# A memory pair's fetches in one step, and its gate's tanh ordered behind an exponential

## The chip, the core and the metric

The kernel runs on one core of a Trainium2 chip. Five engines work side by side: TensorE (PE, matrix products; its weight loads are shown apart as PEld), VectorE (DVE), ScalarE (ACT), GpSimd (POOL) and SyncE (SP), which here only issues DMAs. Each engine takes its instructions from its own queue, in the queue's order. The metric is the device time of one launch in microseconds (us); the median of three runs of the kernel before is 2737.72 us, from 2735.97 to 2738.56.

## The reference

One layer of a hybrid encoder for a prompt of 2048 rows and for 8 decode requests of 16 rows, all of width 1024, in float32. What is computed:

```python
h = rms_norm(x, norm_g[0]);  z = h @ w_in
qa, ka, va, qb, kb, vb, ob, ib, fb = split(z)
att = rms_norm(band_attention(qa, ka, va, rel_table), g_att)      # 8 heads x 64
hb, (c1, n1, m1) = mlstm_sequence(qb, kb / sqrt(128), vb, ig, log_sigmoid(fb), c0, n0, m0)
hb = hb * rsqrt(mean(hb * hb, -1) + EPS)                          # 4 heads x 128
mlstm_out = hb * g_mlstm * sigmoid(ob)
x = x + rms_norm(concat(att, mlstm_out) @ w_out, norm_g[1])
x = x + rms_norm(conv_ffn(rms_norm(x, norm_g[2])), norm_g[3])
```

The part around the change is the mLSTM, a matrix memory `C` (128 x 128 for each head, with a normaliser column) that is carried from chunk to chunk. For each chunk the weights are exp(d - m), with d from the gates and m a running maximum; the chunk's result is its own part, `(q k^T * w) v`, plus the carried part, `q C`; and `C` is scaled and gets `(k w_s)^T v`. At the end each head's row is normalised and multiplied by its gain and by the output gate sigmoid(ob), which the kernel computes as (1 + tanh(ob / 2)) with the gain halved.

## The kernel before

**Stages.** First the combined projection: 14 column groups of `w_in` for the first half of the rows (prompt tiles 0 to 7 and the decode tile), then the same 14 for the second half (tiles 8 to 15). A float32 product is made of three products of rounded and residual parts (`mm3`, L111 to L113). Groups `va`, `qk` give the attention's values, queries and keys, groups `qb`, `vo` the memory's queries and keys (`qkbd` in DRAM) and its values and output gates (`vobd`). Then comes the output projection (`project`, L997 and on), whose rows are read back from `mixd` in DRAM (L1015), squared and summed (L1020), scaled (L1022) and transposed (L83), and then the feed-forward part, which takes the second half of the time. Its matrix products have their sums and products of blocks arranged so that seven take the place of eight; nothing of the change lies in it.

**Units beside the projection.** Attention and memory run in the gaps of the projection's products. Each is a stream of units, and a unit is a Python generator that issues some instructions at each step and yields an estimate of their cost. A `Pipe` (L155 and on) holds the live units of one stream; one step of a pipe starts the next unit, if any, and lets every live unit issue its next step. `pump` (called after every few projection products) steps the attention's pipe and the memory's pipe in turn as long as the estimated VectorE cost lags behind.

**The memory's units.** `mlstm(h, half)` treats one head and one half of the rows: 8 chunks of 128 rows in 4 pairs. For each pair there are `chunk(s, 0)`, `load` of the pair after it, `chunk(s, 1)` and an empty unit. With 4 heads and 2 halves there are 32 pairs and 64 chunks.

`load` (L690 to L706) has three steps. The first takes the tile `mb` and fetches the running maximum, broadcast to all partitions (L693). The second takes the tile `mqk` and fetches queries and keys (L697), takes the tile `mvo` and fetches values and output gate (L700), writes a column of ones into `mvo` on GpSimd (L701) and masks `mb` on GpSimd (L702). The third loads the head's gain, for the first pair only. The tiles `mb`, `mqk`, `mvo`, `num` have two buffers each.

`chunk(s, c)` (L708 to L741): the first step makes q k^T (L715) and the transposed keys (L83), the exponential of the masked `mb` on ScalarE into `w` (L718), the scaled keys `kw` on ScalarE (L720), and `w` times the scores on VectorE (L721). The second step has the three products (L727 to L729), the carried memory's update on VectorE (L730) and the pair's `num` on ScalarE and VectorE (L731, L732). After the second chunk a third step calls `finish_heads`.

`finish_heads` (L662 to L684): the norms (squares on ScalarE, L671; the power on GpSimd, L676), the output gate's tanh in place on ScalarE (L677), gate times gain on VectorE (L678), the normalised and gated rows on VectorE (L682, which is the last reader of `mvo`), and their store to `mixd` on SP's queue (L684).

`mlstm_sample(h)` treats the decode rows of a head in its own units `own`, `batches` and `finish`; the last calls `finish_heads` too, so that there are 32 + 4 tanhs.

**What sets the order.** The whole program is written under

```python
with tile.TileContext(nc, schedule_with_timeline_sim=True) as tc:
```

so the order in which the code issues is not the order of the queues. A planner takes the instructions with their dependences, gives those that the code issues earlier the higher rank, simulates the engines with its own durations, and puts into each engine's queue whatever is ready in its simulation. Instructions of different units so change places, and a DMA whose buffer is not yet released is planned for the time when it will be. Once planned, a queue's order is fixed, and the chip keeps to it: an instruction whose data are late holds up all behind it on its queue. The code can add edges: `keep_in_program_order` (in use before) and `issue_after` (new, below).

The loads of weights (L1256), attention inputs (L356 to L380), rows (L1015, L1042), the loads of the memory's pairs and most stores share SP's queue.

Of the kernel before, what the change touches and what calls it, by code (L numbers as in the profile page):

```python
# [12 lines left out]
AF = mybir.ActivationFunctionType  # L13
# [37 lines left out]
def hymba_step(ctx: ExitStack, tc: tile.TileContext, I: dict, O: dict):  # L51
# [607 lines left out]
        yield 0.3, 0.8  # L659


    def finish_heads(num, enm, og, h, nch, dst, name):  # L662

        den = num[:, :, 0]
        ad = small.tile([P, 2], F32, tag="ad", name=f"ad{name}")[:, :nch]
        ssq = small.tile([P, 2], F32, tag="mssq", name=f"mssq{name}")[:, :nch]
        nc.vector.scalar_tensor_tensor(ad, den, -1.0, den, op0=ALU.mult, op1=ALU.max)
        nc.vector.tensor_tensor(ad, ad, enm, op=ALU.max)
        for c in range(nch):
            jk = pm.tile([P, P], F32, tag="wexp", name=f"jk{name}_{c}", bufs=2)  # L670
            nc.scalar.activation(jk, num[:, c, 1:DH + 1], AF.Square, accum_out=ssq[:, c:c + 1])  # L671
        nc.vector.tensor_tensor(ad, ad, ad, op=ALU.mult)
        nc.vector.scalar_tensor_tensor(ad, ad, DH * EPS, ssq, op0=ALU.mult, op1=ALU.add)
        f = small.tile([P, 2], F32, tag="mf", name=f"mf{name}")[:, :nch]
        nc.gpsimd.tensor_scalar(ad, ad, 1.0 / DH, 0.0, op0=ALU.mult, op1=ALU.add)
        nc.gpsimd.tensor_tensor(f, ad, nhalf[:, :nch], op=ALU.pow)  # L676
        nc.scalar.activation(og, og, AF.Tanh, scale=0.5)  # L677
        nc.vector.scalar_tensor_tensor(og, og, 1.0,  # L678
                                       hgm[h].unsqueeze(1).broadcast_to([P, nch, DH]),
                                       op0=ALU.add, op1=ALU.mult)  # L680
        for c in range(nch):
            nc.vector.scalar_tensor_tensor(num[:, c, 1:DH + 1], num[:, c, 1:DH + 1], f[:, c:c + 1], og[:, c, :],  # L682
                                           op0=ALU.mult, op1=ALU.mult)
        nc.sync.dma_start(dst, num[:, :, 1:DH + 1])  # L684

    def mlstm(h, half):
# [3 lines left out]
        def load(s):  # L690
# [1 line left out]
            s.mb = pm.tile([P, 2, P], F32, tag="mb", name=f"mb{s.nm}", bufs=2)  # L692
            nc.sync.dma_start(s.mb, md.rearrange("(c h) t -> h c t", c=8)[h:h + 1, 2 * s.pc:2 * s.pc + 2]  # L693
                              .broadcast_to([P, 2, P]))
            yield 0.0, 0.0
            s.qk = pm.tile([P, 2, 256], F32, tag="mqk", name=f"mqk{s.nm}", bufs=2)
            nc.sync.dma_start(s.qk, qkbd[h][sg][:, :, o * P:o * P + 256])  # L697
            vo = pm.tile([P, 2, 2 * DH + 1], F32, tag="mvo", name=f"mvo{s.nm}", bufs=2)
            s.va, s.og = vo[:, :, 0:e], vo[:, :, e:]
            nc.sync.dma_start(vo[:, :, 1:], vobd[h][sg][:, o:o + 2, :])  # L700
            nc.gpsimd.memset(vo[:, :, 0:1], 1.0)  # L701
            nc.gpsimd.affine_select(out=s.mb, in_=s.mb, pattern=[[0, 2], [1, P]], compare_op=ALU.is_ge, fill=BIG,  # L702
                                    base=0, channel_multiplier=-1)
# [5 lines left out]
        def chunk(s, c):  # L709
# [5 lines left out]
            nc.tensor.matmul(sp[:, 0:P], k_, q_, start=True, stop=True)  # L715
            transpose(sp[:, P:2 * P], k_)
            w = pm.tile([P, P], F32, tag="wexp", name=f"w{s.nm}_{c}", bufs=2)
            nc.scalar.activation(w, s.mb[:, c, :], AF.Exp, bias=col(0), scale=-1.0)  # L718
            kw = pm.tile([P, P], F32, tag="kw", name=f"kw{s.nm}_{c}", bufs=2)
            nc.scalar.activation(kw, sp[:, P:2 * P], AF.Identity, scale=col(3))  # L720
            nc.vector.tensor_tensor(w, sp[:, 0:P], w, op=ALU.mult)  # L721
# [12 lines left out]
            if c == 0:  # L734
# [1 line left out]
            r0 = 2 * s.pc * HB + h  # L736
            sg, o = s.t0 // 4, s.t0 % 4
            finish_heads(num, cols[:, 2, r0:r0 + HB + 1:HB], s.og, h, 2,
                         mixd[sg][:, o:o + 2, 512 + h * DH:512 + (h + 1) * DH], s.nm)
            if half == 1 and s.pc == 3:  # L740
                nc.sync.dma_start(O["c_prompt"][h], cst[h])  # L741
            yield 0.0, 1.3
# [11 lines left out]
    def mlstm_sample(h):  # L754
# [6 lines left out]
        def own():  # L761
# [19 lines left out]
            w = pm.tile([P, P], F32, tag="wexp", name=f"w{nm}", bufs=2)  # L781
            nc.scalar.activation(w, s.mb, AF.Exp, bias=col(0), scale=-1.0)
            s.kw = pm.tile([P, P], F32, tag="kw", name=f"kw{nm}", bufs=2)
            nc.scalar.activation(s.kw, sp[:, P:2 * P], AF.Identity, scale=col(3))
            nc.vector.tensor_tensor(w, sp[:, 0:P], w, op=ALU.mult)
            yield 0.32, 0.2
            acc = ps_me(f"ma{nm}")
# [30 lines left out]
        def finish():  # L818
            yield 0.0, 0.0
            yield 0.0, 0.0  # L820
            finish_heads(s.num, cols[:, 2, h:h + 1], s.og, h, 1, mixs[:, h * DH:(h + 1) * DH].unsqueeze(1), nm)
            yield 0.0, 0.8

        yield FLUSH
# [1199 lines left out]
```

## Time and profile before

| | |
|---|---|
| median of three runs | 2737.72 us (2735.97 to 2738.56) |
| the profiled execution | 2736.37 us |
| its span, first to last instruction | 2734.6 us |
| instructions | 47676 |
| mean granted clock of TensorE | 0.993 |
| TensorE busy | 2652.1 us (97%) |
| VectorE busy | 1862.9 us (68%) |
| ScalarE busy | 1418.7 us (52%) |
| GpSimd busy | 685.8 us (25%) |

The page of the profile gives busy times, the chain of waits that ended last, and the costliest groups of instructions. A row of a group reads: line, engine, operation, out<-in by the program's tile names, shapes, count, then busy time, mean duration in ns, and the engine's idle time just before these instructions with what ended it. A row of a timeline reads: start in us from the span's start, duration, engine, line, operation, tiles, and in square brackets the idle time before it with what ended it. A row of the waits reads: who waited, for what, us in total, number of times, the longest. A row of windows reads: the window, its length, then for PE, PEld, DVE, ACT and POOL the busy time with the number of instructions, then TensorE's granted clock, the DMA engines' share and GB/s. In the view of one tile, a row of instructions gives the least, median and greatest duration in ns and the first and the last start; the indented rows give what ended the engines' idle time before them, with us in total and times. SPq is SP's queue of DMAs. The tile that holds values and output gate is called `mvo`, the one with queries and keys `mqk`, the masked maximum `mb`, the rows of the output projection `mr`, the chunk's products `ms`.

### The profile page before, as it was taken

What the parts mean: (1) busy time and instruction counts of PE and PEld (TensorE: products, weight loads), DVE (VectorE), ACT (ScalarE), POOL (GpSimd) and SP (SyncE); (2) the same over time, 40 slices, a digit from 0 to 9 for tenths busy, and PEclk for the clock granted to TensorE, in tenths of its full rate; (3) what the DMA queues carried; (4) which work ended last, traced back from release to release, by engine and by line L of the source; (5) the groups of instructions that cost most, each with busy time, mean ns of one, the idle gap of its engine ahead of it and who ended that gap; (6) DMA issues with size and microseconds to landing.
All of it is one profiled execution on the core that took longest, in us unless ns stands there. A gap on an engine that the chain in (4) does not pass through costs nothing.

```text
span 2734.6 us, 47676 instructions
## 1 busy us (share of the span) xinstructions
PE 2652.1 (97%) x16459; PEld 2476.5 (91%) x16459; DVE 1862.9 (68%) x3519; ACT 1418.7 (52%) x2904; POOL 685.8 (25%) x1325
## 2 busy tenths in 40 slices
PE   7999999999999999999999999999999999999998
PEld 7899989998999998777999997789999878999976
DVE  4445455533556666466899997758888875999956
ACT  4445554433556665333545456655454665555554
POOL 1000001101100001254444542013333212456401
PEclk9999999999999999999999999999999999999999
DMA  5545465558544544588777668767886877798875
GB/s 170 149 128 150 127 186 153 158 158 269 179 141 127 159 140 156 176 293 289 285 232 239 204 200 284 244 191 199 227 215 179 251 240 243 212 247 235 256 256 183
DMA packets 333856, 555.74 MB, mean 203 GB/s; under 512 B 61906, under 2 KB 169518, under 8 KB 333294
## 3 DMA queue, kind: packets, MB, share of 16 engines
q1 hardware_dynamic: 250942, 405.06, 48.1%
q0 software_dynamic: 44080, 113.81, 14.3%
q10 hardware_dynamic: 38592, 33.83, 3.7%
q8 instruction: 129, 2.11, 0.3%
q14 instruction: 113, 0.93, 0.1%
HBM read 390.03 MB, written 172.22 MB: 206 GB/s over the span
## 4 chain that ended last, share of the span: by engine, by line
PE 45%; DVE 3%; DMA 3%; issue 1%; ACT 1%; POOL 0%; DVEq 0%; POOLq 0%; SPq 0%; ACTq 0%
PE uec L111 6%; PE uec L112 6%; PE uec L113 6%; PE dn L113 4%; PE dn L111 4%; PE dn L112 4%; PE ua L113 3%; PE ua L112 3%; PE ua L111 3%; PE dnm L113 2%; PE ub L113 1%; PE dnm L112 1%; PE ub L111 1%; PE ub L112 1%; PE dnm L111 1%
## 5 line engine op out<-in xcount | busy, mean ns | idle before, releaser
L111 PE MATMUL uec<-B,wuh 128*128 128x384 f32 (+1 forms) x720 | 236.0, 328 | 6.4 <-DVE ug L1523 4.7
L112 PE MATMUL uec<-B,wuh 128*128 128x384 f32 (+1 forms) x720 | 235.1, 327 | 0.0
L113 PE MATMUL uec<-B,wul 128*128 128x384 f32 (+1 forms) x720 | 234.4, 327 | 0.0
L1352 ACT CAST wuh<-wu 128x512 fp32r<-128x512 f32 x255 | 141.7, 618 | 113.1 <-PE uec L112 110.8
L113 PE MATMUL dn<-wdh,al 128*128 128x512 f32 x462 | 186.1, 403 | 3.5 <-DVE al L1353 3.4
L111 PE MATMUL dn<-wdh,ah 128*128 128x512 f32 x462 | 183.4, 397 | 5.9 <-ACT ah L1352 3.9
L1353 DVE TENSOR_TENSOR al<-ar,ah 128x768 fp32r<-128x768 f32 (+2 forms) x141 | 108.4, 779 | 117.8 <-ACT ah L1352 115.5
L112 PE MATMUL dn<-wdl,ah 128*128 128x512 f32 x462 | 182.7, 395 | 0.0
L1352 ACT CAST ah<-ar 128x768 fp32r<-128x768 f32 (+2 forms) x141 | 96.1, 692 | 151.5 <-PE dnm L112 112.3
L1353 DVE TENSOR_TENSOR wul<-wu,wuh 128x512 fp32r<-128x512 f32 x255 | 164.3, 683 | 2.4 <-ACT wuh L1352 2.4
L111 PE MATMUL vo<-wi_h,hT 128*128 128x256 f32 x544 | 156.9, 288 | 2.1 <-ACT qb_st L246 2.1
L113 PE MATMUL vo<-wi_h,hT 128*128 128x256 f32 x544 | 156.1, 287 | 0.0
L112 PE MATMUL vo<-wi_l,hT 128*128 128x256 f32 x544 | 155.4, 286 | 0.0
L1353 DVE TENSOR_TENSOR wdl<-wdr,wdh 128x512 fp32r<-128x512 f32 x231 | 145.3, 684 | 8.3 <-ACT wdh L1352 5.9
L111 PEld LDWEIGHTS uec<-B,wuh 128*128 128x128 f32 x720 | 135.1, 188 | 9.4 <-issue 4.9
L423 ACT ACTIVATE tmp<-tmp,mn 128x640 f32<-128x640 f32 (+4 forms) x128 | 97.6, 762 | 84.4 <-DVE mn L422 73.0
L422 DVE CUSTOM_DVE_ANT_0 tmp<-s,nb 128x640 f32<-128x640 f32 (+4 forms) x128 | 94.2, 736 | 61.8 <-PE s L412 61.1
L112 PEld LDWEIGHTS uec<-B,wuh 128*128 128x128 f32 x720 | 135.2, 188 | 0.2
L113 PEld LDWEIGHTS uec<-B,wul 128*128 128x128 f32 x720 | 135.1, 188 | 0.0
L1352 ACT CAST wdh<-wdr 128x512 fp32r<-128x512 f32 x231 | 127.5, 620 | 12.9 <-PE uec L112 7.6
L435 DVE TENSOR_TENSOR ptl<-pt,pth 128x640 fp32r<-128x640 f32 (+4 forms) x128 | 93.6, 737 | 58.6 <-ACT pth L434 57.7
L111 PE MATMUL qk<-hT,wi_h 128*128 128x384 f32 (+1 forms) x384 | 130.0, 339 | 0.5 <-ACT gates L293 0.5
(473 smaller groups left out, 8968.1 us busy)
## 6 DMA issues: line engine op xcount, KB each, us to landing
wu<-in_w_up SPq DMA_DIRECT2D x220, 256.0 KB, 4.9
wu<-wsd SPq DMA_DIRECT2D x176, 256.0 KB, 4.9
wdr<-wtd SPq DMA_DIRECT2D x132, 256.0 KB, 5.3
wi_raw<-in_w_in SPq DMA_DIRECT2D x52, 512.0 KB, 4.5
wdr<-in_w_down SPq DMA_DIRECT2D x99, 256.0 KB, 4.5
wsd<-ws POOLq DMA_DIRECT2D x88, 256.0 KB, 4.7
ar<-ad_S SPq DMA_DIRECT2D x50, 384.0 KB, 4.5
kraw<-kTd SPq DMA_DIRECT2D x112, 128.0 KB, 3.1
```

Of the source, the lines that this page charges most:

```text
L111: nc.tensor.matmul(out, ah, bh, start=start, stop=False, skip_group_check=onto)
L112: nc.tensor.matmul(out, ah, bl, start=False, stop=False, skip_group_check=onto)
L113: nc.tensor.matmul(out, al, bh, start=False, stop=stop, skip_group_check=onto)
L422: nc.vector.tensor_tensor_reduce(o_, s_, b_, 1.0, 3e38, ALU.add, ALU.min, accum_out=mn)
L423: nc.scalar.activation(tmp[:, :n], tmp[:, :n], AF.Exp, bias=mn, scale=-1.0, accum_out=rsum[:, i % 4, hh:hh + 1])
L435: nc.vector.tensor_tensor(s.ptl[:, sl, qc], ptv, s.pth[:, sl, qc], op=ALU.subtract)
L1352: nc.scalar.copy(h, r)
L1353: nc.vector.tensor_tensor(l, r, h, op=ALU.subtract)
```

## The change

The change has two parts. In `load`, the step's end (`yield 0.0, 0.0`) between the fetch of `mb` and the fetches of `mqk` and `mvo` moves behind them, so that the first step takes the three tiles and issues the three fetches, and the second has the column of ones and the mask; the number of steps stays three. The decode units' loading stays as it is.

In `chunk`, the ScalarE instruction of the exponential is kept as `s.mark`; the second chunk's overwrites the first's. `finish_heads` gets it as an argument, and the gate's tanh is issued inside `tc.issue_after(mark.ins)`: each instruction in that block gets an order-only edge (no semaphore) behind the given one on the same engine's queue. For the decode rows the mark is the scaling of the keys.

```diff
-    def finish_heads(num, enm, og, h, nch, dst, name):
+    def finish_heads(num, enm, og, h, nch, dst, name, mark):
...
-        nc.scalar.activation(og, og, AF.Tanh, scale=0.5)
+        with tc.issue_after(mark.ins):
+            nc.scalar.activation(og, og, AF.Tanh, scale=0.5)
...
             nc.sync.dma_start(s.mb, md.rearrange("(c h) t -> h c t", c=8)[h:h + 1, 2 * s.pc:2 * s.pc + 2]
                               .broadcast_to([P, 2, P]))
-            yield 0.0, 0.0
             s.qk = pm.tile([P, 2, 256], F32, tag="mqk", name=f"mqk{s.nm}", bufs=2)
             nc.sync.dma_start(s.qk, qkbd[h][sg][:, :, o * P:o * P + 256])
             vo = pm.tile([P, 2, 2 * DH + 1], F32, tag="mvo", name=f"mvo{s.nm}", bufs=2)
             s.va, s.og = vo[:, :, 0:e], vo[:, :, e:]
             nc.sync.dma_start(vo[:, :, 1:], vobd[h][sg][:, o:o + 2, :])
+            yield 0.0, 0.0
             nc.gpsimd.memset(vo[:, :, 0:1], 1.0)
...
-            nc.scalar.activation(w, s.mb[:, c, :], AF.Exp, bias=col(0), scale=-1.0)
+            s.mark = nc.scalar.activation(w, s.mb[:, c, :], AF.Exp, bias=col(0), scale=-1.0)
...
-                         mixd[sg][:, o:o + 2, 512 + h * DH:512 + (h + 1) * DH], s.nm)
+                         mixd[sg][:, o:o + 2, 512 + h * DH:512 + (h + 1) * DH], s.nm, s.mark)
...
-            nc.scalar.activation(s.kw, sp[:, P:2 * P], AF.Identity, scale=col(3))
+            s.mark = nc.scalar.activation(s.kw, sp[:, P:2 * P], AF.Identity, scale=col(3))
...
-            finish_heads(s.num, cols[:, 2, h:h + 1], s.og, h, 1, mixs[:, h * DH:(h + 1) * DH].unsqueeze(1), nm)
+            finish_heads(s.num, cols[:, 2, h:h + 1], s.og, h, 1, mixs[:, h * DH:(h + 1) * DH].unsqueeze(1), nm, s.mark)
```

## The prediction

> **What bounds the kernel now.** I read the page's head first, then a sum over the stage in which the memory's units run beside the projections, then the waits around the tile that the change touches, then the timelines where TensorE stood still.
>
> ```profile
> span 2734.6 us, 47676 instructions
> ...
> PE 2652.1 (97%) x16459; PEld 2476.5 (91%) x16459; DVE 1862.9 (68%) x3519; ACT 1418.7 (52%) x2904; POOL 685.8 (25%) x1325
> ```
>
> The profiled execution took 2736.4 us, 1.8 of it around the span of 2734.6; the median of the three runs shown is 2737.7, so I add 1.3 us to what I work out on the profiled execution. TensorE is busy for 97% of the span. ScalarE is half idle, so ScalarE's time as such is worth nothing: the change can only give what TensorE's idle time around the memory's units gives, or what a slow clock behind such idle time gives. The stage runs from about 250 to 1200 us:
>
> ```profile
> 250.00:1200.00 950.00, 923.63 (x6857) 874.63 (x6856) 510.24 (x1260) 477.49 (x1206) 117.19 (x295) 0.99 0.55 168
> ```
>
> The second column is the length, the third TensorE's busy time: 950.00 - 923.63 = 26.4 us of idle time. That is the ceiling, but for the clock. The tile with the gate (`mvo`: value and output gate of a chunk pair) shows what the change is about:
>
> ```profile
> L718 ACT ACTIVATE w<-mb,colsp x64: 384/402/416, 116.7 to 1164.4; 128x128 f32<-128x128 f32 x64
> ...
> L700 SPq DMA_DIRECT2D mvo<-vobd x32: 360/421/862, 275.9 to 1146.2; - x32
> L677 ACT ACTIVATE mvo<-mvo x32: 406/421/422, 278.6 to 1149.8; 128x256 f32<-128x256 f32 x32
> L678 DVE SCALAR_TENSOR_TENSOR mvo<-mvo,hgm x32: 415/426/429, 279.0 to 1150.2; 128x256 f32<-128x256 f32 x32
> ...
>   ACT mvo L677: 68.3, 30
>   DMA mvo<-vobd: 62.5, 30
> ...
> DMA to landing us min/median/max: 3.1/4.2/7.4
> ```
>
> The tanh (L677) runs 2.7 us after its fetch is issued for the first pair, though the code has it in the pair's last step: the planner has put it where it expects the data to land. The data land later, so ScalarE stands before 30 of the 32 tanhs, 62.5 us in all, and VectorE before the gate's product (L678), 68.3 us. Does TensorE feel it? Here is the worst place, ScalarE, VectorE, GpSimd and TensorE by time, then two windows with the clock:
>
> ```profile
> 1121.26 0.19 ACT L1058 ACTIVATION_READ_ACCUMULATOR mt<-wo 128x1 f32 x1
> 1125.77 0.42 ACT L677 ACTIVATE mvo<-mvo 128x256 f32<-128x256 f32 x1 [4.31 <-DMA mvo<-vobd]
> 1126.09 0.62 ACT L1020 ACTIVATE mt<-mr 128x512 fp32r<-128x512 f32 x1
> ...
> 1126.22 0.43 DVE L678 SCALAR_TENSOR_TENSOR mvo<-mvo,hgm 128x256 f32<-128x256 f32 x1 [5.15 <-ACT mvo L677]
> 1128.95 0.48 DVE L1022 TENSOR_SCALAR mr<-mr,att_rs 128x512 f32<-128x512 f32 x1
> ...
> 1127.69 0.54 POOL L100 TENSOR_TENSOR att_rs<-att_ms,nhalf 128x1 f32<-128x1 f32 x1
> ...
> 1129.48 0.74 PE L83 MATMUL mT_pt<-ident,mr 128*128 128x128 f32 x4 [2.88 <-DVE mr L1022]
> 1130.54 0.80 PE L715 MATMUL ms<-mqk 128*128 128x128 f32 x2 [0.32 <-DVE num L732]
> ```
>
> ```profile
> 1130.00:1136.75 6.75, 6.43 (x20) 4.85 (x19) 2.66 (x6) 2.21 (x6) 2.42 (x5) 0.50 0.77 242
> 1136.75:1143.00 6.25, 6.25 (x32) 5.18 (x31) 2.30 (x8) 2.90 (x10) 1.08 (x3) 1.00 0.72 236
> ```
>
> This is one chain. ScalarE is free at 1121.45 and waits 4.31 us for the gate's data; queued behind that tanh is the sum of squares of a row that has nothing to do with the memory (L1020); behind it the reciprocal root on GpSimd (L100), the scaling on VectorE (L1022), and the transposes of TensorE, which stands 2.88 us. Then the clock in the window's seventh figure is 0.50 for 6.75 us: half of that, 3.4 us, is lost again.
>
> **The tanh's new place.** What it removes: no instruction. 36 tanhs (32 of 0.42 us, 4 of 0.31 for the decode heads) run as before, each with an order-only edge behind the pair's second exponential on the same queue (for a decode head, behind the keys' scaling). The edge adds a wait where that exponential is late; then the pair's gate product and its final product (L682) queue behind it on VectorE. How much room is there? One pair's second exponential, and the store of its heads:
>
> ```profile
> 1115.75 0.40 ACT L718 ACTIVATE w<-mb,colsp 128x128 f32<-128x128 f32 x1
> ...
> 1145.73 0.37 SPq L684 DMA_DIRECT2D mixd<-num  x1
> ```
>
> Thirty us, against 0.42 + 0.43 for tanh and gate product: the edge costs nothing. Without that room it would cost these 0.85 us a pair in the pair's finish. What it gives is read where TensorE stood behind a tanh's wait. Besides the place above there are five, each with the tanh on ScalarE and the TensorE row it ended in:
>
> ```profile
> 287.71 0.42 ACT L677 ACTIVATE mvo<-mvo 128x256 f32<-128x256 f32 x1 [2.77 <-DMA mvo<-vobd]
> ...
> 656.70 0.42 ACT L677 ACTIVATE mvo<-mvo 128x256 f32<-128x256 f32 x1 [1.74 <-DMA mvo<-vobd]
> ...
> 982.06 0.42 ACT L677 ACTIVATE mvo<-mvo 128x256 f32<-128x256 f32 x1 [3.95 <-DMA mvo<-vobd]
> ...
> 1062.11 0.42 ACT L677 ACTIVATE mvo<-mvo 128x256 f32<-128x256 f32 x1 [1.36 <-DMA mvo<-vobd]
> ...
> 1105.53 0.42 ACT L677 ACTIVATE mvo<-mvo 128x256 f32<-128x256 f32 x1 [6.43 <-DMA mvo<-vobd]
> ```
>
> ```profile
> 289.47 0.66 PE L83 MATMUL pt<-ident,tmp 128*128 128x128 f32 x4 [0.49 <-ACT tmp L423]
> ...
> 657.83 0.38 PE L715 MATMUL ms<-mqk 128*128 128x128 f32 x1 [1.13 <-DVE num L732]
> ...
> 984.24 0.38 PE L447 MATMUL ot<-pth,vhl 128*128 128x256 f32 x1 [0.51 <-ACT pth L434]
> ...
> 1064.45 0.39 PE L447 MATMUL ot<-pth,vhl 128*128 128x256 f32 x1 [0.41 <-ACT pth L434]
> ...
> 1111.57 0.66 PE L83 MATMUL mT_pt<-ident,mr 128*128 128x128 f32 x4 [0.98 <-DVE mr L1022]
> ```
>
> Together 0.49 + 1.13 + 0.51 + 0.41 + 0.98 = 3.5 us. ScalarE's waits behind them (1.4 to 6.4 us) are each longer than TensorE's, so in principle all of it goes; but other work stands directly behind, and I take half, 1.8. At 1129 I take all: the row's load was issued at 1114.46 (its line stands below), long before; ScalarE was free at 1121.45, and 4.31 us earlier is more than 2.88. That is 2.88 + 0.32 + 3.4 = 6.6 us. The bounds of this part are 0 and 3.5 + 6.6 = 10.1 us.
>
> **The fetches' new place.** In each of the 32 loads two DMAs on SP's queue (L697 for queries and keys, L700 for values and gate) and the two tile allocations move one step forward in the code, past whatever the attention's unit and the weight loading issue in between on SP; the mask and the column of ones stay on GpSimd. Where they stand in the queue today:
>
> ```profile
> 1100.92 0.37 SPq L684 DMA_DIRECT2D mixd<-num  x1
> 1101.33 0.47 SPq L700 DMA_DIRECT2D mvo<-vobd  x1
> ...
> 1113.82 0.53 SPq L697 DMA_DIRECT2D mqk<-qkbd  x1
> 1114.46 0.53 SPq L1015 DMA_DIRECT2D mr<-mixd  x1
> ```
>
> ```profile
> SPq L697 <- PE ms L729: 61.3, 16, 9.3
> ```
>
> The gate's fetch leaves directly behind the store of the pair two before it, that is, when one of its two buffers comes free; the queries' fetch waits in the queue for the last products (L729) of the pair two before. Buffers time both, not the step in the code, and their number stays two. So I expect the fetches at the same times and take 0. The bounds: a fetch that now goes one step earlier can land up to a step earlier, but after the first part nothing waits for the gate's landing, so the gain's bound is 0 as well; the loss's is below, with the rival on the other side.
>
> **The sum.** 2736.4 - 6.6 - 1.8 + 0 = 2728.0 us against the profiled execution, 2729.3 against the median. I predict 2729.
>
> [...]
>
> ```profile
> 774.43 0.38 PE L111 MATMUL vo<-wi_h,hT 128*128 128x256 f32 x1 [2.07 <-ACT qb_st L246]
> ...
> 775.00:778.40 3.40, 3.40 (x18) 3.40 (x17) 2.60 (x5) 3.40 (x9) 0.63 (x2) 0.51 0.87 252
> ```
>
> **Rivals.** (1) *Another wait takes the place*, no change by measure. The planner orders every engine's queue from its own simulated times, and it plans anew with 36 tanhs elsewhere; waits for other DMAs stay in the queues, such as the one that ends at 774.43, which has no tanh before it. If one new gap of that kind comes (2.07 and half of 3.4, 3.8 us) or the row at 1129 keeps half of its wait, 8.4 - 3.8 = 4.6 remain: 2733. For it: only 10.1 of the stage's idle time and clock loss hang on a tanh at all. Against it: at 1129 no other late thing shows.
>
> (2) *The clock comes back without the gap*, that is, its fall at 1130 had a cause other than the 2.88 us and stays: the gain is 8.4 - 3.4 = 5.0, 2732.7. [...] Against it stand the two places above.
>
> (3) *The early fetches block SP*, slower. The queries' fetch waits up to 9.3 us in SP's in-order queue. One step earlier it can be planned ahead of a row's load (L1015, now 0.6 us behind it). That row landed, by the 4.2 us median of the gate's fetch, at about 1118.7 (an estimate); ScalarE could have used it at 1121.45. So from about 2.8 us of blocking on the sum of squares is late and TensorE stands as at 1129: 6.6 us an event. Three events outweigh the gain: 2737.7 - 8.4 + 19.8 = 2749. For it: SP's longest wait there is three times that slack. Against it: the fetch stands ahead of that load already, and buffers, not code, time it.
>
> (4) *More than the rows named*: VectorE is rid of its 68.3 us too, and gaps too small for my list shrink. If as much again comes as the 10.1, the time is 2737.7 - 20.2 = 2717.5.
>
> **How the numbers follow.** A difference under 0.2%, 5.5 us, can't be told from no change here: the bounds are 2732.2 and 2743.2. My forecast has 0.47, of which 0.07 ends above 2732.2 because more than the half taken is handed on; (1) has 0.27, (2) 0.05, (3) 0.13, (4) 0.08. Faster: 0.40 + 0.08 = 0.48. No change: 0.07 + 0.27 + 0.05 = 0.39. Slower: 0.13. The range goes down to (4), 2717, and up to one event of (3) with no gain left, 2737.7 + 6.6 = 2744; beyond that lie the worse half of (3) and little of (4). The forecast's own range is 2727.6 (all 10.1) to 2733.
>
> **What would show it.** In the changed profile the tanh's row (L677's successor) has no idle time before it for the fetch, but for a pair whose exponentials run long before its fetch lands, as the first pair's do at 116.7; ScalarE's 62.5 us falls under 15, and VectorE's 68.3 with it. Around the rows' transposes at about 1130 the gap and the 0.50 are gone. The gate's fetch still leaves right behind a store. TensorE's idle time from 250 to 1200 falls from 26.4 to about 21. I am wrong if the tanhs' waits go and TensorE's idle time does not, if a clock of 0.50 appears elsewhere in that stage, or if SP's wait for the products (61.3) grows and rows or weights land late.

## The result, and the profile after

The changed kernel takes 2731.77 us (median), the kernel before beside it 2738.14: a ratio of 0.9974, 95% interval 0.9964 to 0.9984, or 6.4 us less by the medians (4.4 to 9.9 by the interval). The forecast was 2729, the range 2717 to 2744, and "faster by over 0.2%" had the greatest chance. Single executions of one kernel scatter with a standard deviation of 5.0 us (before) and 5.7 us (changed), so most of what follows is read from places in the traces, and only the sums from the times. The profiled execution took 2730.95 us. Its page's head:

```profile
span 2729.2 us, 47644 instructions
...
PE 2651.2 (97%) x16459; PEld 2474.6 (91%) x16459; DVE 1862.9 (68%) x3519; ACT 1421.0 (52%) x2904; POOL 692.4 (25%) x1325
```

The work is the same (16459 products, 2904 instructions on ScalarE; the 32 fewer in the total are of the kind that is not counted as busy). TensorE's busy time fell by 0.9 us only: what went is its idle time, 2734.6 - 2652.1 = 82.5 us before and 2729.2 - 2651.2 = 78.0 now. The mean granted clock is 0.993 in both profiles. The view of the tile with values and gate, which before had 62.5 us of ScalarE's and 68.3 us of VectorE's waits:

```profile
L678 ACT ACTIVATE mvo<-mvo x32: 401/407/424, 276.4 to 1161.0; 128x256 f32<-128x256 f32 x32
L679 DVE SCALAR_TENSOR_TENSOR mvo<-mvo,hgm x32: 407/426/445, 276.8 to 1161.5; 128x256 f32<-128x256 f32 x32
...
  ACT mvo L678: 17.2, 15
...
  DMA mvo<-vobd: 7.2, 2
```

The tanh (now L678) waits for its fetch twice, 7.2 us, and the gate's product behind it 17.2 us in all. The two are pairs whose exponentials run long before their fetch lands (at 114 and 780 us, their tanhs at 276 and 792), as the forecast had said of the first. Next the place at 1129 of the forecast; the timeline of all engines there, and the windows over it:

```profile
1119.23 0.37 SPq L685 DMA_DIRECT2D mixd<-num  x1
1119.70 0.42 SPq L700 DMA_DIRECT2D mvo<-vobd  x1
...
1122.19 0.19 ACT L1059 ACTIVATION_READ_ACCUMULATOR mt<-wo 128x1 f32 x1
...
1122.42 0.63 ACT L1021 ACTIVATE mt<-mr 128x512 fp32r<-128x512 f32 x1
...
1125.29 0.48 DVE L1023 TENSOR_SCALAR mr<-mr,att_rs 128x512 f32<-128x512 f32 x1
...
1127.37 0.60 PE L83 MATMUL mT_pt<-ident,mr 128*128 128x128 f32 x4
...
1128.54 0.49 PE L716 MATMUL ms<-mqk 128*128 128x128 f32 x2 [0.57 <-DVE num L733]
```

```profile
1120.30:1123.71 3.41, 3.41 (x18) 2.81 (x17) 0.98 (x2) 1.78 (x5) 2.14 (x7) 1.00 0.89 172
1123.71:1127.12 3.41, 3.41 (x20) 2.86 (x18) 1.68 (x2) 0.00 (x1) 0.87 (x2) 1.00 1.02 402
1127.12:1130.54 3.42, 2.70 (x17) 2.00 (x16) 2.55 (x6) 2.77 (x7) 0.95 (x3) 1.00 0.41 127
```

The row's squares (L1021) run directly behind ScalarE's sums, with no tanh between; the scaled row is ready at 1125.8, 1.6 us before its transposes come up in TensorE's queue at 1127.37, where before TensorE stood 2.88 us. What is left is 0.57 us, and the clock (seventh figure) stays at 1.00 where it was 0.50 for 6.75 us.

Not all went so. The same stage has a gap that the kernel before did not have. Timeline of the changed kernel, then the windows from the one with the gap on:

```profile
554.80 0.80 DVE L885 COPY held<-held 64x64 f32<-64x64 f32 x4 [3.10 <-DMA held<-qTd]
555.63 0.29 DVE L733 TENSOR_TENSOR num<-num,ms 128x129 f32<-128x129 f32 x1
...
555.97 0.79 PE L716 MATMUL ms<-mqk 128*128 128x128 f32 x2 [3.04 <-DVE num L733]
```

```profile
552.22:555.64 3.42, 0.71 (x6) 0.50 (x5) 0.77 (x5) 1.22 (x3) 0.28 (x1) 1.00 0.70 231
555.64:559.05 3.41, 3.08 (x14) 3.08 (x15) 1.70 (x3) 0.64 (x3) 0.00 (x0) 0.50 0.06 23
```

VectorE waits 3.10 us for the decode queries' fetch, with the pair's sum (L733) queued behind, and TensorE with its next chunk behind that: 3.04 us, then 3.4 us at half clock (0.50). In the kernel before, VectorE waits at nearly the same place, but other work stands behind, and TensorE loses half as much:

```profile
552.08 1.01 DVE L884 COPY held<-held 64x64 f32<-64x64 f32 x4 [2.79 <-DMA held<-qTd]
...
555.38 0.39 PE L111 MATMUL va<-wi_h,hT 128*128 128x264 f32 x1 [1.53 <-ACT gates L293]
```

So TensorE's busy time from 250 to 1200 did not rise in this execution (923.63 before):

```profile
250.00:1200.00 950.00, 922.57 (x6847) 872.71 (x6845) 510.65 (x1262) 479.52 (x1207) 122.31 (x297) 0.99 0.56 169
```

### The profile page after: what moved, and what is told of

Its sections match the earlier page's. It is cut to its first block, busy times and chain, and to the rows that moved or that the text cites. A ratio compares the mean times of both kernels' runs of the same rounds, so it can differ in the third digit from the quotient of the medians.

```text
span 2729.2 us, 47644 instructions
## 1 busy us (share of the span) xinstructions
PE 2651.2 (97%) x16459; PEld 2474.6 (91%) x16459; DVE 1862.9 (68%) x3519; ACT 1421.0 (52%) x2904; POOL 692.4 (25%) x1325
## 5 line engine op out<-in xcount | busy, mean ns | idle before, releaser
L1353 ACT CAST wuh<-wu 128x512 fp32r<-128x512 f32 x255 | 141.7, 618 | 115.9 <-PE uec L112 113.5
```

The costliest lines, as they stand in the source:

```text
L1353: nc.scalar.copy(h, r)
```

## The experiments

All ratios are against the kernel before, on the same chip, with their 95% intervals; where us are given they are the difference of medians.

### The changed kernel, and each part alone

The whole change again:

> The change as it is, beside its two parts on the same chip. Theory A (the tanh no longer holds ScalarE's queue): some 6 us faster than the kernel before, ScalarE idle before the tanh under 15 us instead of 62.5, no gap of 2.9 us at the rows' transposes near 1130. Theory B (the fetches leave one step earlier) gives the same total. Theory C (any other order of the planner moves the time by some us) has no number of its own for it: between -8 and +8.

Measured: 2727.41 against 2734.55, ratio 0.9981 (0.9968 to 0.9994), 7.1 us less; ScalarE's wait before the tanhs is 10.4 us.

The fetches' move alone (the diff is against the changed kernel):

```diff
-        with tc.issue_after(mark.ins):
-            nc.scalar.activation(og, og, AF.Tanh, scale=0.5)
+        nc.scalar.activation(og, og, AF.Tanh, scale=0.5)
```

> Only the fetches are moved to the first step; the tanh keeps its old freedom. Theory A: no change, within 2 us of the kernel before; ScalarE still idles some 60 us before the tanhs, since buffers time the gate's fetch. Theory B: all of the gain, some 6 us faster, and the wait before the tanhs smaller. Theory C: anything within 8 us to either side.

Measured: 2732.79, ratio 1.0004 (0.9988 to 1.0019): nothing; ScalarE still waits 62.1 us before the tanhs. More telling than the time is the order. Compared instruction by instruction, by line, operation and tile, the queues of this kernel are those of the kernel before on all five engines. Its timeline therefore has the old gap, 2.66 us at its 1124:

```profile
1124.42 0.81 PE L83 MATMUL mT_pt<-ident,mr 128*128 128x128 f32 x3 [2.66 <-DVE mr L1022]
```

The tanh's edge alone (the step's end put back between the fetch of `mb` and the other two):

```diff
+            yield 0.0, 0.0
             s.qk = pm.tile([P, 2, 256], F32, tag="mqk", name=f"mqk{s.nm}", bufs=2)
...
             nc.sync.dma_start(vo[:, :, 1:], vobd[h][sg][:, o:o + 2, :])
-            yield 0.0, 0.0
```

> Only the tanh is ordered behind the second exponential; the fetches stay in the second step. Theory A: all of the gain, 5 to 8 us faster, ScalarE idle before the tanhs under 15 us. Theory B: no change, within 2 us. Theory C: anything within 8 us to either side.

Measured: 2726.50, ratio 0.9976 (0.9963 to 0.9989), 8.0 us less, with 11.2 us of wait before the tanhs; its queues are those of the changed kernel, on all engines. The two parts are settled: the first does nothing, the second is the whole effect.

### How far behind must the tanh stand?

The edge behind the pair's first exponential instead of the second:

```diff
-            s.mark = nc.scalar.activation(w, s.mb[:, c, :], AF.Exp, bias=col(0), scale=-1.0)
+            ex = nc.scalar.activation(w, s.mb[:, c, :], AF.Exp, bias=col(0), scale=-1.0)
+            s.mark = ex if c == 0 else s.mark
```

> As the whole change, but the tanh is ordered behind the pair's first exponential. In the profile of before that exponential ran 1 to 3 us behind the tanh's late start in most pairs, so the gate's data have landed by then. Theory A: the wait before the tanhs is nearly gone too (under 20 us) and the gain is 4 to 8 us, in a third order of the queues. Theory C: a gain or loss that has nothing to do with the wait, anywhere within 8 us.

Measured: 2730.27, ratio 0.9985 (0.9977 to 0.9994), 4.3 us less. The view of the tile gives ScalarE's wait for the fetch:

```profile
  DMA mvo<-vobd: 24.8, 12
```

24.8 us in 12 waits, more than the 20 expected: the first exponential is too early for 12 of 32 fetches. The expectation had misread the old order: there the first exponential runs 1 to 3 us behind the tanh in 11 pairs only, and ahead of it in 12. A kernel with two fifths of the waiting left has kept about half of the gain, but the intervals overlap, and the waits are not all that differs. At the last head this kernel has the longest gap of TensorE in any of the profiles, behind a late `w`, with 13.65 us of half clock after it:

```profile
1162.95 0.80 PE L729 MATMUL ms<-cst,mqk 128*128 128x129 f32 x2 [4.74 <-DVE w L723]
```

So this run shows that the first exponential is too early, and not what each wait costs.

### Where does the gain sit?

The edge on the last head's four pairs alone (the rows at 1129 belong to it), and on all but these:

```diff
-        with tc.issue_after(mark.ins):
+        with tc.issue_after(mark.ins) if name in ("3_8", "3_10", "3_12", "3_14") else ExitStack():
```

(The second kernel has `not in` in place of `in`.)

> The tanh is ordered behind the second exponential for the four pairs of the last head of the second half only, which run between 1098 and 1166 us; the other 28 pairs and the decode heads are as before. Theory A with the prediction's sum: the gap of 2.9 us near 1130 and the clock of 0.50 behind it go, 6.6 us, so this kernel has most of the gain: 5 to 7 us faster than before, and the gap near 555 is the old one (1.5 us, behind the gates' copy). Theory C (luck of the planner's order up to 1090): no change, within 2 us, since that order is the old one.

> The opposite: all tanhs are ordered but those of the last head's four pairs in the second half. TensorE's queue has the order of the changed kernel. Theory A with the prediction's sum: the five smaller places give 1.8 us, the gap near 1130 and its slow clock are back; with the gap near 555 that the changed kernel's profile shows (3.0 instead of 1.5 us, and a slow clock behind it in two of three profiles, 1.7 us) the rest is eaten: 0 to 2 us faster than before. Theory C: as fast as the whole change, since the order up to 1090 is its order: 6 us.

Measured: the last head alone 2731.98 against 2733.95, ratio 0.9993 (0.9979 to 1.0008), 2 us less where 5 to 7 were expected; all but the last 2729.85, ratio 0.9984 (0.9970 to 0.9999), 4 us less where 0 to 2 were. By the times, the forecast had the shares the wrong way round. The last head's kernel was run once more, beside the whole change:

> The change's edge on the last four chunk pairs' tanhs only, once more, since its first comparison (1.9 us faster, interval from 5.7 faster to 2.2 slower) does not tell a half of the gain from nothing. Theory A (the gain sits at the last head's rows, where the steps of the trace give 4.5 us): 3 to 6 us faster than the kernel before. Theory B (the gain is spread over all heads, the last head's part is eaten later): 0 to 2 us faster.

> The changed kernel once more, so that the three below stand beside it on the same chip. Expected as in the first comparison: 5 to 8 us faster than the kernel before. In its profile the gap before the scaled row's transposes (2.9 us at about 1129 in the kernel before) is at most 0.6 us, the gap of 2 to 3 us at about 555 and the one of 2 to 3.6 us at about 1180 (behind the vector engine's waiting fold) are both there. Whether each is followed by a slow clock depends, by the theory of fixed windows of 3.41 us, on whether 1.7 us or more of it fall into one window; by the rival, the length of the gap alone, each gap above 2.0 us is followed by one.

Measured, against 2732.00: 2730.49 for the last head, ratio 0.9985 (0.9970 to 1.0000), 1.5 us less; 2725.17 for the whole, ratio 0.9970 (0.9959 to 0.9980), 6.8 us less. So by the times the last head's edges alone give 1.5 to 2 us of some 7 (theory B's numbers, though the upper bounds of both intervals still hold part of theory A's), and the edges before them the rest.

And yet the place is as forecast. All but the last, timeline with the tanh's wait, the gap, and the window behind it:

```profile
1120.39 0.42 ACT L678 ACTIVATE mvo<-mvo 128x256 f32<-128x256 f32 x1 [4.33 <-DMA mvo<-vobd]
...
1124.11 1.12 PE L83 MATMUL mT_pt<-ident,mr 128*128 128x128 f32 x4 [2.91 <-DVE mr L1023]
```

```profile
1124.50:1131.30 6.80, 6.43 (x22) 4.86 (x21) 2.88 (x6) 2.24 (x6) 2.44 (x5) 0.54 0.73 242
```

The last head alone, same place, only the short gap of the changed kernel:

```profile
1121.54 0.49 PE L716 MATMUL ms<-mqk 128*128 128x128 f32 x2 [0.57 <-DVE num L733]
```

The gap of 2.9 us and the slow clock follow the last head's tanhs exactly. What they are worth is worked out from TensorE's timeline, by counting products of the projection (4752) and the output projection (816), so that each stage holds the same work in every kernel. In brackets stand TensorE's idle time and the loss to half clock, all in us; the loss is an estimate, half the time at 0.50. (By the products' pace it is about a tenth less: in the kernel before those of `vo` follow each other every 0.21 us from 775.05 to 777.83, at 0.50, and every 0.12 us from 768.24 to 770.49, at 1.00.) The stretch ahead of the first row is left out: all nine have the same queues there, and it takes 261.8 to 267.0 us. The columns are nine executions of six kernels:

| stretch | before | fetches alone | changed | whole | whole, again | tanh alone | last head | last head, again | all but last |
|---|---|---|---|---|---|---|---|---|---|
| 1184th to 4564th product of the projection | 739.7 (13.7, 1.7) | 740.7 (15.2, 0) | 741.9 (15.3, 1.7) | 738.0 (11.4, 3.4) | 738.6 (14.4, 0) | 736.7 (12.2, 0) | 738.0 (11.9, 1.7) | 739.3 (15.2, 0) | 737.6 (11.5, 1.7) |
| to the 193rd of the output projection | 113.4 | 112.8 | 114.6 | 112.3 | 114.3 | 112.5 | 113.1 | 114.9 | 113.2 |
| 193rd to 385th (the place at 1129) | 64.8 (6.0, 3.4) | 64.7 (5.8, 3.4) | 60.2 (4.1, 0) | 60.8 (4.7, 0) | 60.1 (4.1, 0) | 60.3 (4.2, 0) | 60.3 (4.2, 0) | 61.0 (5.0, 0) | 64.8 (6.1, 3.4) |
| 385th to 769th | 111.7 (6.3, 1.7) | 113.5 (5.3, 5.1) | 112.8 (5.1, 5.1) | 115.3 (7.7, 3.4) | 111.4 (5.8, 1.7) | 113.4 (7.2, 1.7) | 115.5 (9.0, 3.4) | 117.4 (8.4, 5.1) | 114.5 (7.3, 3.4) |
| to the end | 1438.0 | 1436.4 | 1435.2 | 1433.9 | 1434.7 | 1434.0 | 1433.6 | 1435.9 | 1435.7 |

The third row divides the nine executions cleanly: 64.7 and 64.8 where the last head's tanhs stand as before, 60.1 to 61.0 where they have the edge. That is 3.7 to 4.7 us in one place. In the fourth row the two executions of the last head alone have the longest times of all nine, 115.5 and 117.4 against 111.7 and 113.5 of the old order: most of the 4.4 us (by which the third row's means differ) is lost again there, although TensorE's and SP's queues are identical in all nine kernels from 1120 us on. The largest piece of it in the second of them:

```profile
1183.60 0.80 PE L113 MATMUL wo<-wo,mt 128*128 128x512 f32 x1 [2.54 <-DVE mt L219]
```

```profile
1182.67:1189.50 6.83, 5.90 (x14) 4.65 (x15) 4.22 (x9) 0.00 (x0) 6.24 (x12) 0.50 0.93 363
```

That is 2.54 us and, by the same estimate, half of 6.83. The same gap is there in the old order too, and how long it is, and how long the clock stays at 0.50, changes from execution to execution (2.18 us and 3.41 in the kernel before, 2.61 and 6.83 in the changed one). The other rows differ by 1 to 5 us between executions of identical queues (the four from "changed" to "tanh alone"), so a gain of 1.4 us in the projection (740.2 in the mean of the first two, 738.8 of those four) is plausible and not proved by them.

### Can the new gaps be taken away?

The second run of the whole change settles half of its own expectation: the gap at about 1180 is shorter than expected (1.74 us); the one at about 555 is there (2.82 us) and no slow clock follows it, against the rival by length; but a window with only 3.42 - 1.85 = 1.57 us idle is followed by one, below the 1.7 of the other theory. Its rows stand in the last section, with what all the profiles together say.

In all profiles of the changed order VectorE's wait for the decode queries ends in the gap at about 555. The queries' copies were put behind older VectorE instructions (of a list of nine recent ones, the oldest):

```diff
...
-                nc.vector.tensor_copy(z[rr, :, hh * DS:(hh + 1) * DS], qf[rr, :, b * DS:(b + 1) * DS])
+                with tc.issue_after(dmark[0].ins) if b < b0 + 2 else ExitStack():
+                    nc.vector.tensor_copy(z[rr, :, hh * DS:(hh + 1) * DS], qf[rr, :, b * DS:(b + 1) * DS])
...
```

> The whole change, and the decode attention's first two copies of the queries are ordered behind an older VectorE instruction (the ninth last of three kinds), so that they leave the place where VectorE stands 3.1 us for their data at 551 to 555 us with a memory pair's sum behind them. Theory A: the gap of 2.3 to 3.0 us near 555 and the slow clock behind it go, 3 to 4.5 us faster than the whole change, 9 to 11 us faster than before. The rival: the place is taken by the gates' copy as before the change (1.5 us), or the decode attention becomes late, and nothing is gained over the whole change.

Measured: 2728.11, ratio 0.9968 (0.9955 to 0.9980), 5.8 us less. The gap at 555 is gone, but this profile has two others, each with a window of half clock behind it:

```profile
668.15 0.49 PE L718 MATMUL ms<-mqk 128*128 128x128 f32 x2 [1.62 <-DVE num L735]
...
693.13 1.11 PE L83 MATMUL spt<-ident,stmp 128*128 128x128 f32 x4 [2.56 <-ACT stmp L907]
```

In this profile nothing is won in the projection's stage (740.1 us by the table's first row), and by the times it can't be told from the whole change. The profile is one execution, though. The last two kernels below have the same copies, and up to 1107 us the same queues as this one: in the one neither gap is above 1 us, in the other a single one of 1.60 us stands at 690, and their first rows take 735.2 and 734.9 us. So the two gaps need not come with the copies. The mean of the three (736.7) against that of the five profiles with the whole change's queues up to there (738.4) would be a gain of 1.7 us, inside the scatter of the row.

The second recurrent gap lies at 1171 to 1188 us in the old order and the new (in all profiles but that of the first exponential). Timeline of the changed kernel:

```profile
1183.19 0.69 DVE L1213 TENSOR_TENSOR fold<-fold,fold 128x512 f32<-128x512 f32 x1 [2.40 <-issue]
...
1183.87 1.22 DVE L219 TENSOR_TENSOR mt<-mT_pt,mt 128x1024 fp32r<-128x1024 f32 x1
...
1185.14 0.79 PE L113 MATMUL wo<-wo,mt 128*128 128x512 f32 x1 [2.61 <-DVE mt L219]
```

`folds` (the sums and differences of blocks of the down weights, on VectorE, with fetches on GpSimd's queue) is kept in program order; one of its rows waits 2.40 us, and behind it stands the residual of a transposed row (L219) that TensorE waits for. I took the waiting row for the fold's second difference and gave its fetch a step more:

```diff
             if old:
+                make(k - 1, 1, 2, 1, sub)
                 make(k - 1, 2, 0, 2, sub)
...
-            make(k, 1, 2, 1, sub)
             yield
```

> The whole change, and the second difference of each fold of the down weights (the vector engine's row that waits 2.0 to 2.4 us for its fetch at about 1180) put one step later in the fold's own order, so that its fetch has three steps instead of two. Theory (that wait holds the row of the normalization behind it, and TensorE with it): the fold's wait falls under 1 us, TensorE's gap of 2 to 3.6 us at 1175 to 1190 goes or falls under 1.2 us, with the slow clock behind it; 2 to 6 us faster than the whole change. Rival (the planner puts another waiting transfer there, or the fetch is late by more than a step): the gap stays above 1.5 us or another comes within 40 us, and the time is that of the whole change within 2 us.

> Both additions on the whole change: the folds' second difference a step later, and the decode queries' copies ordered behind the ninth last of the vector engine's older rows. If each takes away its own gap (about 555 and about 1180) and nothing comes in its place: 4 to 10 us faster than the whole change. If the gaps only move, as the queries' addition alone did (two gaps of 1.6 and 2.6 us at 668 and 693 for the one at 555): the time is that of the folds' addition alone within 2 us.

Measured, beside the second run of the whole change (2725.17): the fold's step alone 2725.03, ratio 0.9973 (0.9958 to 0.9989), no gain; with the queries' copies 2722.03, ratio 0.9965 (0.9950 to 0.9980), 3 us below the whole change, which the intervals do not separate. The theory fell for the fold. Its timeline:

```profile
1173.27 0.69 DVE L1213 TENSOR_TENSOR fold<-fold,fold 128x512 f32<-128x512 f32 x1 [2.36 <-issue]
...
1173.95 1.22 DVE L219 TENSOR_TENSOR mt<-mT_pt,mt 128x1024 fp32r<-128x1024 f32 x1
```

The same wait, 2.36 us, at the same place: counted in VectorE's queue, four rows to a fold, this row is the fold's last sum (with the fourth part), not the second difference. I had moved the wrong row. The profile names no releaser for it ("issue"), but the trace has the landing of the fourth part's fetch: 1183.11 us in the changed kernel and 1173.19 here, each 0.08 us before the row starts. The last run moved the right one, on top of both:

```diff
                 store(k - 1, (0, 1))
-                make(k - 1, 3, 3, 2, plus)
             yield
             if old:
+                make(k - 1, 3, 3, 2, plus)
                 store(k - 1, (2, 3))
```

> Both additions as in the run before, and the fold's sum with its fourth part put one step later as well. In the queue of the vector engine the row that waits 2.4 us ahead of the normalization's scaled transposes (at about 1183 in the changed kernel, 1173 with the second difference later) is this sum, not the second difference, which the last run moved in vain. Theory (the sum waits for the fourth part's fetch, and TensorE behind it): the gap of 2.0 to 3.6 us at 1170 to 1190 falls under 1.2 us, no slow clock follows it, and the kernel is 2 to 5 us faster than with both additions, that is 10 to 14 us faster than the kernel before. Rival (the planner lays the wait elsewhere, or another fetch is late there): the gap stays above 1.5 us or another of that size comes within 40 us, and the kernel is 7 to 10 us faster than the kernel before, as with both additions.

Measured: 2720.22 against 2729.09, ratio 0.9966 (0.9956 to 0.9976), 8.9 us less. Timeline:

```profile
1174.41 0.69 DVE L1216 TENSOR_TENSOR fold<-fold,fold 128x512 f32<-128x512 f32 x1 [1.09 <-DMA fold<-in_w_down]
...
1177.22 0.72 DVE L1216 TENSOR_TENSOR fold<-fold,fold 128x512 f32<-128x512 f32 x1 [0.99 <-DMA fold<-in_w_down]
1177.86 1.21 DVE L221 TENSOR_TENSOR mt<-mT_pt,mt 128x1024 fp32r<-128x1024 f32 x1
...
1179.13 0.50 PE L113 MATMUL wo<-wo,mt 128*128 128x512 f32 x1 [1.40 <-DVE mt L221]
```

The sum is the row at 1174.41; it waits 1.09 us, now put down to the fetch, and no longer stands ahead of the residual. In its place stands the next fold's first difference (1177.22), which waits 0.99 us for a fetch of its own, and TensorE's gap is 1.40 us. That is less than the old gap and more than the 1.2 expected, a window of half clock still follows, and another gap of 1.47 us came at 1121. By the table's count the stretch from the 385th to the 769th product takes 109.3 us, less than in any of the nine, that from the 193rd to the 385th 62.1 instead of about 60. The time falls to the rival's 7 to 10 us. This kernel's median is the lowest of all that were run, but so is that of the kernel before beside it: the ratio is the one of both additions without the sum (0.9965), and its interval overlaps the whole change's 0.9959 to 0.9980. That any of the three additions gains is not shown by the times.

## Why the prediction was right, and where not

**The direction and the mechanism: right.** The tanh's edge alone is 8.0 us faster (0.9963 to 0.9989), and where the last head's tanhs get it, the gap of 2.9 us and the half clock at about 1129 go, every time. The chain from tanh to squares to reciprocal root to scaled row to transposes was the one on TensorE's path. That the total came within 3 us of the forecast is in part luck: one term was too large, the other by the times too small (below).

**The fetches' move at nothing: right,** and the trace agrees with the stated reason. Not even a queue's order changed, and in the changed kernel the gate's fetch at 1119.70 still follows at once on a store (of the pair two before, at 1119.23). The rival of the early fetches that block SP had no ground, since the fetches alone change nothing. But one of its signs appeared with the tanh's edge, which re-plans SP's queue too. SP's wait for the products grew from 61.3 to 80.9 us (81.5 with the edge alone):

```profile
SPq L697 <- PE ms L730: 80.9, 18, 8.3
```

No wait for a row of the output projection came of it. But rows of the prompt (`xr`, the input of the projection) and the projection's weights did land later for ScalarE. A timeline of the changed kernel, then ScalarE's wait for the weights before and after:

```profile
541.49 1.06 ACT L236 ACTIVATE hT<-xr 128x1024 fp32r<-128x1024 f32 x1 [4.92 <-DMA xr<-in_x_prompt]
...
544.93 1.09 PE L83 MATMUL hT_pt<-ident,xr 128*128 128x128 f32 x8 [1.54 <-DVE xr L239]
```

```profile
ACT wi_h L1262 <- DMA wi_raw<-in_w_in: 44.9, 25, 3.4
...
ACT wi_h L1263 <- DMA wi_raw<-in_w_in: 56.9, 27, 5.1
```

Between 400 and 700 us TensorE waits 2.8, 1.4, 2.2 and 1.4 us for such rows in the four profiles with all edges, and 0 and 0.2 us in the first two columns of the table. So the third of the forecast's signs of being wrong came in part as well, by the tanh's edge and not by the fetches: it is a price of the new order, and the 6.4 us are what is left after it.

**The edge at nothing: right.** ScalarE's waits went from 62.5 to 7.2 us (under 15 forecast), VectorE's from 68.3 to 17.2 (the forecast's "with it", under 15, is just missed). The room is there in every pair: its final product (L682) starts at least 17.0 us behind the second exponential before, and at least 17.8 after.

**The term at 1129: right in kind, too large in size.** Forecast 6.6 us, "2.88 + 0.32 + 3.4". By the table it is 3.7 to 4.7. The clock's 3.4, an estimate as half of some 6.8 us at 0.50 (about 3.0 by the products' pace), came back in full: no slow clock is left there. The idle time fell only by 1 to 2 us instead of 3.2, since 0.57 us stay at the same spot and a new short gap opens behind it, 0.62 us at 1142.83. My "I take all" left out what is late next.

```profile
1142.83 0.66 PE L83 MATMUL mT_pt<-ident,mr 128*128 128x128 f32 x4 [0.62 <-DVE mr L1023]
```

**The five other places, 1.8 us: too small by the times.** All but the last head is 4.1 us faster (ratio 0.9984, by its interval 0.3 to 8.2 us); the forecast gave it 1.8, with a bound of 3.5. The table's first row accounts for 1.4 us in the mean. Where the remainder is, stays open: the stages' scatter between executions of the same queues is as large. Nor does any run separate these tanhs' own waits from the rest of the new plan, which changes the order on all five engines, TensorE's from 286 to 1091 us; only at 1129, where TensorE's and SP's queues are the old ones, is the tanh's place shown to be the cause.

**TensorE's idle time from 26.4 to about 21: wrong in this profile,** 950.00 - 922.57 = 27.4. With that, and with a clock of 0.50 at 555 that was not there before, two more of the forecast's own signs of being wrong appeared. A fixed window does not hold the same work in both, but by equal work (first, third and fourth rows of the table) the idle time also falls only from 26.0 and 26.3 us to between 23.6 and 24.5, two and not five. The step that failed is the same one, that nothing takes the place of the removed waits: rival (1) came true in part, with the gap at 555 (3.04 us and 1.7 of clock, against 1.53 before). It was named as one new gap of 3.8 us and takes, with half of 3.41 us at 0.50 as the estimate of the clock's part, 3.04 - 1.53 + 1.7 = 3.2 more than before. The second run of the whole change has 950.00 - 924.34 = 25.7 and the same gap at 2.82 without the slow clock, so part of that cost is not fixed. On the other side, the wait at 774 (2.07 us and 1.7 of clock before), which the prediction counted among those that stay, is 1.84 us at 786 in the changed profile, without a slow clock.

**The clock's rival** (that its fall at 1130 has another cause) is out: it falls to 0.50 where the gap is, in the three profiles of the table that have it (2.66 to 2.91 us), and in none of the six without. **Rival (4),** twice the bound, is out too: the interval ends at 9.9 us.

**The sum.** Forecast 8.4 us, measured 6.4 with 6.8 and 7.1 in the two repeats. In the table's terms (mean of the four executions with all edges against the first two): 4.4 less at 1129, 1.4 less in the projection, 0.3 and 0.6 more in the second and fourth rows, and 2.8 less in the last row, where all queues are the same. That last difference belongs to no step of the change that I can name; with it the sum is 7.7, without it 4.9, and the measured 6.4 lies between. The forecast's 6.6 + 1.8 had the first term too large; whether the second was too small is as uncertain as the last row.

## What to carry to other kernels

Where a planner orders in-order queues by its own durations, a cheap instruction that waits for a DMA is set where the planner believes the data to be; look for the unrelated work queued behind it, for that is where the loss was, and an edge without a semaphore behind something known to be late enough cost nothing here (ScalarE's waits before the tanhs fell from 62.5 to 7.2 us, and each final product still starts at least 17.8 us behind the second exponential). Each such move re-plans all queues, so compare the orders, stage by stage over equal counts of work, before believing a gain or a loss, and identify a waiting row by its operands before moving it. A part of a change that leaves all queues as they were, as the fetches did here (ratio 1.0004, 0.9988 to 1.0019), needs no timing at all.

## What the runs showed of the hardware

**What goes with a fall of the clock in these 14 profiles is TensorE's idle time within a fixed window, not the length of a gap.** In every profile the stretches of half clock begin on a grid of 3.413 us (in the kernel before, for example, at 774.94, 1129.93 and 1187.95 us, 104 and 17 steps apart) and last one or two of its steps (four behind the gap of 4.74 us; the one at the launch's end is cut off). The second run of the whole change, windows cut on that grid:

```profile
1050.46:1053.88 3.42, 1.85 (x12) 1.38 (x11) 2.98 (x7) 2.15 (x6) 2.62 (x6) 1.00 1.01 354
1053.88:1057.29 3.41, 3.41 (x18) 3.41 (x17) 1.81 (x4) 1.56 (x5) 0.00 (x0) 0.50 0.81 312
...
552.12:555.53 3.41, 1.66 (x13) 1.66 (x14) 2.42 (x7) 1.07 (x3) 0.00 (x0) 1.00 0.55 182
555.53:558.94 3.41, 3.41 (x31) 3.41 (x30) 0.35 (x1) 0.80 (x4) 0.00 (x0) 1.00 0.23 77
...
1176.76:1180.17 3.41, 1.32 (x4) 0.60 (x4) 1.86 (x5) 2.36 (x7) 0.93 (x2) 1.00 0.90 199
1180.17:1183.58 3.41, 2.83 (x7) 2.25 (x8) 2.63 (x6) 0.00 (x0) 2.88 (x7) 0.50 1.03 408
```

The gap of 2.82 us at 553.87 is cut by a window's edge: 3.41 - 1.66 = 1.75 us of it lie in the window, and the next window runs at 1.00. At 1176.76 two shorter gaps give 3.41 - 1.32 = 2.09 us, and the next window has 0.50. With the folds a step later, the same gap at 552 is 3.26 us long, and 2.74 of it lie in one window:

```profile
549.49:552.91 3.42, 0.68 (x5) 0.68 (x6) 1.78 (x6) 0.39 (x2) 0.00 (x0) 1.00 0.52 173
552.91:556.32 3.41, 3.41 (x18) 3.41 (x17) 0.65 (x2) 0.77 (x3) 0.00 (x0) 0.50 0.14 48
```

3.42 - 0.68 = 2.74 us idle, then 0.50. Over the 14 profiles (before, after and all those above), from 40 us on and without the last 25 us, so counted for windows that are themselves at full clock: of 10624 with under 1.2 us idle none is followed by half clock; of 81 with 1.2 to 1.6, 4 are (one of them the 1050.46 window above, 1.57); of 30 with 1.6 to 1.8, 12; of 24 with 1.8 to 2.0, 20; and of 52 with 2.0 and more, all. Ordered by the length of single gaps, there is no such line: of 20 gaps of 2.0 to 2.5 us 16 have a window at half clock at them, of 12 of 3.0 to 3.5 us 10. By the windows, a little over half of 3.41 us idle was enough; from 1.2 to 2.0 us both happen, and the ends of the products are modelled in the profiles, so a sharp line is not shown. Why some falls last two windows, as behind the 2.88 us (6.83 us), and others one, as behind the 2.07 us at 774 (3.41), I could not settle.

So gaps of 2.5 to 3 us had no slow clock behind them (2.82 us at about 555 in the second run of the whole change), 3.41 us of it (3.04 us at the same place in the changed kernel) or 6.83 (2.54 us at about 1183 in the second run of the last head): by the estimate of half the time at 0.50 they cost nothing more, 1.7 us more or 3.4 us more. Where the grid lies in the span differs between the executions: the edges of its windows near 555 us are at 555.64 in the changed kernel, 555.53 in the second run of the whole change and 556.32 with the folds a step later. With about four gaps of 2 us and more in a launch (55 in 14 profiles) that would be, by estimate, a scatter of a few microseconds between executions of one kernel, near the size that the times show (standard deviations of 5.0 and 5.7 us); that it is their main cause was not tested.
